# Seven products of quarters for the retention gate, with its operand sums made beside the state-space batches

## The chip, the cores and the metric

The kernel runs on one core of a Trainium2 chip. Time is device microseconds of one execution. The engines are named as in the profile: PE (TensorE matmul), PEld (its weight load), DVE (VectorE), ACT (ScalarE), POOL (GpSimd), and SP, whose queue issues most of the DMA transfers.

## What is computed

Two layers on x of 1024 frames and 1024 channels. The change touches layer 0 only: one input projection `w_in` gives the state-space input u, its gate g_s5, q, k, v and the retention gate g_ret; the two branches are gated and projected back.

```python
h = rmsnorm(x, norm_g[0])
u_s5, g_s5, q, k, v, g_ret = jnp.split(h @ w_in, cuts, axis=-1)
y_s5 = s5_mixer(u_s5, ...)            # diagonal complex recurrence, then a GLU
y_s5 = y_s5 * jax.nn.silu(g_s5)
y_ret = retention(q, k, v) * jax.nn.silu(g_ret)
x = x + jnp.concatenate([y_s5, y_ret], axis=-1) @ w_out
```

Layer 1 is a convolution module of its own, and a last rmsnorm follows.

## The kernel before, in words

All products are made from split operands: a float32 value is a high part in a rounded format (`wh`, `xh`) and the remainder (`wl`, `xl`), and `mm3` (L264) adds three matmuls, high by high, high by low and low by high. A weight block of 1024 x 128 takes one DMA, one cast on ACT (L260) and one subtraction for the low part (L261); the set `LO_V` says for which blocks that subtraction is on DVE, all others are on POOL. Weights are taken in the order of `plan`, two blocks ahead (`wnext`), and have three buffers each for `wf`, `wh` and `wl`. The tiles of x, scaled by the norm's weights, stay in SBUF as 16 pairs `xh`, `xl`: 8 blocks of channels (the depth of the products) by two halves of 512 frames. The norm's factor per frame is in the tile R and is multiplied in when a result leaves its bank.

In `layer0_front` the blocks of u come first. Then 16 blocks of gate (g8 to g15 for the state space, g16 to g23 for the retention) are interleaved with eight state-space batches, two blocks to a batch. A gate block is 2 x 24 matmuls into two PSUM banks, a product with R on DVE, a Silu on ACT and a store. A batch B is, on PE: the input products v (L971), the kernel products kp (L980, L982), and the outputs y of the batch before (L1053, L1057). POOL makes its tables ahead of time (`s5_tables`: Tc and Ts, rotations, and W3, powers; L871 to L873, 12 operations a batch); W3 has two buffers, so its writing waits for the outputs of two batches before. DVE makes the weights W2 of the input products and runs the recurrence; kernel and outputs go through DRAM (`k_d`, `y_d`). Behind the gate come the key, query and value projections (k0, q0, v), which read the 16 pairs of x again.

The order of instructions on an engine is a scheduler's, which puts a ready instruction into a gap; `ORDER` and `s5_order` pin pairs of instructions. On the chip each engine takes its queue strictly in that order. `glu_sums` and `y_pass` (retention stage) already do for the GLU product what the change does for the gate.

Of the kernel before, what the change touches and what calls it, by code (L numbers as in the profile page):

```python
# [19 lines left out]
P = 128  # L20
# [69 lines left out]
def s5_order():  # L90

    seq = []
    for b in range(8):
# [7 lines left out]
        seq += [*kern, *turns, *z[:6]] if b else [*turns, *z[:6], *kern]  # L101
        if b:
# [3 lines left out]
        seq += [(f"gt_{h}", 0), *([(f"wl_g{g + 2}", 0)] if b < 7 else []), (f"gt_{h}", 1)]  # L106
    return [*(("Activation", (f"pw0_{b + 1}", 0), (f"gt_{8 + 2 * b}", 0)) for b in range(1, 7)),
# [15 lines left out]
def nat(ap):  # L123

    return ap.rearrange("p (a c) -> p a c", a=LANES)
# [16 lines left out]
class Trunk:  # L142
# [22 lines left out]
    def plan(self):  # L165
# [4 lines left out]
        seq += [(A["w_ab"][nb], f"g{nb}") for nb in range(8, 24)]  # L170
        for p in range(4):
            seq += [(A["w_ab"][28 + p], f"k{p}"), (A["w_ab"][24 + p], f"q{p}")]
# [6 lines left out]
        quad = lambda i, j, m: A["w_glu"][i, m, :, j]  # L179
        sums = lambda n, m: self.ws_d[n // 2, m, :, n % 2]  # L180
# [110 lines left out]
    def run(self):  # L291
# [29 lines left out]
        self.x1_d = dt("x1_d", [D, T])  # L321

# [28 lines left out]
    def layer0_front(self, st):  # L351
# [155 lines left out]
        self.s5_tables(0)  # L507
        for nb in range(8, 24):
# [7 lines left out]
            w = self.wnext(f"g{nb}")  # L516
            with self.tc.issue_after(self.s5_turn.ins) if nb % 2 == 0 and B else nullcontext():
                gate_block(nb, w, self.gs_d if nb < 16 else self.gr_d)
# [139 lines left out]
    def s5_params(self, sp, tp):  # L658
# [27 lines left out]
        prm = load("s5_prm", (3, NP))  # L686
# [163 lines left out]
        self.bb = [sp.tile([P, NP, 16], F32, name=f"s5_bb{c}") for c in "ri"]  # L850
# [27 lines left out]
    def s5_turned(self, pool):  # L878
# [9 lines left out]
        t = self.mid.tile([P, 4, P], F32, name="turned")  # L888
# [177 lines left out]


# [928 lines left out]
def layout(inp):  # L1996
# [7 lines left out]
    order = np.concatenate([w[:, 0:1024][:, s5p], w[:, 1024:2048][:, s5p], w[:, 4096:5120], w[:, 2048:3072]],  # L2004
                           axis=1)
    A["w_ab"] = _blocks(order)
    A["w_u01"] = np.ascontiguousarray(A["w_ab"][:2].reshape(2, P, 2, 4, P).transpose(2, 1, 3, 0, 4)).reshape(2, P, KB, P)
# [49 lines left out]
```

## Time and profile before

| | us |
|---|---|
| three runs | 1121.92, 1123.55 (median), 1124.43 |
| the profiled execution | 1123.15 |
| its span, first to last instruction | 1121.3 |
| eight batches with their gate blocks | 90.30 to 307.50 |

The trace is of one execution, so its time stands beside the span: 1.85 us lie outside it. A line of the timeline has start, duration, engine, source line, operation, output <- input; a line of the grouped view has the count, busy time and mean ns, then the idle time of the engine before them and who ended it. Matmuls overlap: a busy time of 0.38 us is not their pace, which is read from their starts.

### The profile page before, as it was taken

What the parts mean: (1) busy time and instruction counts of PE and PEld (TensorE: products, weight loads), DVE (VectorE), ACT (ScalarE), POOL (GpSimd) and SP (SyncE); (2) the same over time, 40 slices, a digit from 0 to 9 for tenths busy, and PEclk for the clock granted to TensorE, in tenths of its full rate; (3) what the DMA queues carried; (4) which work ended last, traced back from release to release, by engine and by line L of the source; (5) the groups of instructions that cost most, each with busy time, mean ns of one, the idle gap of its engine ahead of it and who ended that gap; (6) DMA issues with size and microseconds to landing.
All of it is one profiled execution on the core that took longest, in us unless ns stands there. A gap on an engine that the chain in (4) does not pass through costs nothing.

```text
span 1121.3 us, 17174 instructions
## 1 busy us (share of the span) xinstructions
PE 1111.2 (99%) x6254; PEld 976.4 (87%) x6254; DVE 822.5 (73%) x1483; ACT 496.6 (44%) x729; POOL 593.5 (53%) x410
## 2 busy tenths in 40 slices
PE   9999999999999999999999999999999999999997
PEld 8888888888888889989888888888888888888886
DVE  7886877666527469587679433599999899999744
ACT  7313333333233231333456424455535677446773
POOL 3049975552145253232573110689544468779863
PEclk9999999999999999999999999999999999999999
DMA  8346755554498676859998997666678655357965
GB/s 323 114 132 181 212 184 174 174 177 145 137 305 294 232 230 175 314 171 349 395 383 290 358 311 268 219 214 210 234 255 298 244 176 183 123 189 233 331 230 182
DMA packets 125445, 261.99 MB, mean 234 GB/s; under 512 B 19760, under 2 KB 49328, under 8 KB 124720
## 3 DMA queue, kind: packets, MB, share of 16 engines
q1 hardware_dynamic: 121376, 248.04, 65.8%
q10 hardware_dynamic: 3984, 12.85, 3.0%
q8 instruction: 49, 0.80, 0.3%
q14 instruction: 36, 0.29, 0.1%
HBM read 182.53 MB, written 74.12 MB: 229 GB/s over the span
## 4 chain that ended last, share of the span: by engine, by line
PE 90%; DVE 3%; DMA 2%; ACT 2%; issue 1%; SPq 1%; POOL 0%; POOLq 0%; ACTq 0%; DVEq 0%
PE mm_g L271 7%; PE mm_g L272 7%; PE mm_g L273 7%; PE mm_wo L271 5%; PE mm_wo L273 5%; PE mm_wo L272 5%; PE mm_b L272 2%; PE mm_a L272 2%; PE mm_a L271 2%; PE mm_b L271 2%; PE mm_b L273 2%; PE mm_a L273 2%; PE mm_u L273 2%; PE mm_u L271 2%; PE mm_u L272 2%; PE mm_glu L271 2%
## 5 line engine op out<-in xcount | busy, mean ns | idle before, releaser
L1669 DVE SCALAR_TENSOR_TENSOR cv<-u,convw,cv 128x512 f32<-128x512 f32 x390 | 267.9, 750 | 6.0 <-ACT cv L1636 3.9
L1630 POOL TENSOR_TENSOR tp<-tp,tp 128x512 f32<-128x512 f32 x64 | 82.3, 1287 | 33.5 <-ACT tp L1629 32.6
L271 PE MATMUL mm_g<-xh,wh_g 128*128 128x512 f32 x256 | 97.7, 382 | 0.0
L272 PE MATMUL mm_g<-xl,wh_g 128*128 128x512 f32 x256 | 97.0, 379 | 0.0
L273 PE MATMUL mm_g<-xh,wl_g 128*128 128x512 f32 x256 | 95.9, 379 | 0.0
L533 POOL TENSOR_TENSOR s1q<-s1q,s1q 128x512 f32<-128x512 f32 x12 | 17.4, 1447 | 81.2 <-ACT s1q L528 81.2
L1629 ACT ACTIVATE tp<-u,convw 128x512 f32<-128x512 f32 x64 | 45.3, 718 | 31.4 <-POOL tp L1630 30.5
L273 PEld LDWEIGHTS mm_g<-xh,wl_g 128*128 128x128 f32 x256 | 48.4, 189 | 6.9
L271 PEld LDWEIGHTS mm_g<-xh,wh_g 128*128 128x128 f32 x256 | 48.4, 189 | 6.8 <-issue 0.2
L272 PEld LDWEIGHTS mm_g<-xl,wh_g 128*128 128x128 f32 x256 | 48.4, 189 | 6.7
L482 DVE TENSOR_TENSOR gt<-mm_g,R 128x512 f32<-128x512 f32 x32 | 21.9, 686 | 43.7 <-PE mm_g L273 43.7
L272 PE MATMUL mm_oc<-zl,wh_woc 128*128 128x512 f32 (+1 forms) x144 | 51.4, 357 | 0.2 <-DVE zl L1384 0.2
L273 PE MATMUL mm_oc<-zh,wl_woc 128*128 128x512 f32 (+1 forms) x144 | 51.0, 357 | 0.0
L271 PE MATMUL mm_oc<-zh,wh_woc 128*128 128x512 f32 (+1 forms) x144 | 51.0, 363 | 0.0
L271 PE MATMUL mm_g<-h1h,wh_cg 128*128 128x512 f32 x128 | 48.9, 382 | 0.0
L271 PE MATMUL mm_wo<-ysh,wh_wos 128*128 128x512 f32 x128 | 48.9, 382 | 0.0
L273 PE MATMUL mm_b<-h1h,wl_cb 128*128 128x512 f32 x128 | 48.5, 379 | 0.0
L271 PE MATMUL mm_a<-h1h,wh_ca 128*128 128x512 f32 x128 | 48.5, 379 | 0.0
L273 PE MATMUL mm_g<-h1h,wl_cg 128*128 128x512 f32 x128 | 48.5, 379 | 0.0
L272 PE MATMUL mm_wo<-ysl,wh_wos 128*128 128x512 f32 x128 | 48.5, 379 | 0.0
L273 PE MATMUL mm_wo<-ysh,wl_wos 128*128 128x512 f32 x128 | 48.5, 379 | 0.0
L272 PE MATMUL mm_a<-h1l,wh_ca 128*128 128x512 f32 x128 | 48.5, 379 | 0.0
(524 smaller groups left out, 3517.7 us busy)
## 6 DMA issues: line engine op xcount, KB each, us to landing
wf_g<-w_ab SPq DMA_DIRECT2D x16, 512.0 KB
wf_wos<-w_out SPq DMA_DIRECT2D x16, 512.0 KB
wf_wor<-w_out SPq DMA_DIRECT2D x16, 512.0 KB
wf_cb<-w_c SPq DMA_DIRECT2D x16, 512.0 KB
wf_ca<-w_c SPq DMA_DIRECT2D x16, 512.0 KB
wf_woc<-w_out_c SPq DMA_DIRECT2D x16, 512.0 KB
wf_v<-w_v SPq DMA_DIRECT2D x12, 512.0 KB
wf_cg<-w_c SPq DMA_DIRECT2D x11, 512.0 KB
```

The costliest lines, as they stand in the source:

```text
L271: nc.tensor.matmul(ps, wh[:, kb, :], xh, start=start, stop=False, **more)
L272: nc.tensor.matmul(ps, wh[:, kb, :], xl, start=False, stop=False, **more)
L273: self.last_mm = nc.tensor.matmul(ps, wl[:, kb, :], xh, start=False, stop=stop, **more)
L482: nc.vector.tensor_tensor(nat(gt[:, c]), un(ps[:]), nat(self.R[:, c]), op=ALU.mult)
L533: nc.gpsimd.tensor_tensor(a, a, sq[:], op=ALU.add)
L1629: nc.scalar.mul(sk[:], u[:, k:k + HALF], cw[:, nb, k:k + 1])
L1630: gp.tensor_tensor(s0[:], s0[:], sk[:], op=ALU.add)
L1669: v.scalar_tensor_tensor(dst[:], *tap, accs_[i][:], op0=ALU.mult, op1=ALU.add)
```

## The change

The retention gate's 1024 x 1024 x 1024 product is cut into quarters (half the channels in, half out, half the frames) and made with seven products of quarters in place of eight, in the form of Strassen and Winograd. Sums of quarters of the weight (four, `gate_sums`, on DVE, during batches 0 to 3) and of quarters of x (four, `x_sums`, on POOL, during batches 1 to 3) are loaded, made and stored to DRAM (`wr_d`, `tx_d`). In batches 4 to 7 `gate_cube` runs 28 quarter products of 12 matmuls, three or four where a gate block stood. Each weight quarter (14 loads, ra to rn) is split like a weight block. Since SBUF has no room for the sums of x beside x itself, `t_load` writes their high and low parts (ACT, POOL) over tiles of x that are not needed any more, through two buffers `tf`, and `restore` loads x again behind the last use and makes both parts anew (ACT, DVE). Partial results are copied to SBUF by ACT (`p1`, `s2`, `s3`), put back into a bank (`us`) for more products to be added to, or added by DVE at the end (`out`).

To make room, three tables of the state space move to pools that are given back early, and the temporary o of `outer` has one buffer. In `s5_order` the pins of the retention gate's steps go. The weights' columns are laid out anew on the host, with the retention gate as its own array `w_gr`.

```diff
@@ plan
-        seq += [(A["w_ab"][nb], f"g{nb}") for nb in range(8, 24)]
+        seq += [(A["w_ab"][nb], f"g{nb}") for nb in range(8, 16)]
+        gr = [q for m in range(2) for q in (quad(0, 0, m), quad(0, 1, m))]
+        gr += [q for m in range(2) for q in (sums(0, m), sums(2, m), quad(1, 1, m))]
+        gr += [sums(n, m) for m in range(2) for n in (3, 1)]
+        seq += [(q, f"r{chr(97 + i)}") for i, q in enumerate(gr)]
@@ layer0_front
+                if 0 < B < 4:
+                    self.x_sums(B - 1)
+                    if B == 3:
+                        self.x_sums(3)
+                if B < 4:
+                    self.gate_sums(B)
-                gate_block(nb, w, self.gs_d if nb < 16 else self.gr_d)
+                if nb < 16:
+                    gate_block(nb, self.wnext(f"g{nb}"), self.gs_d)
+                else:
+                    cube = cube or self.gate_cube(uv)
+                    next(cube)
+            if nb >= 16:
+                for _ in range(3 - nb % 2):
+                    next(cube)
@@ outer
-            t = self.s5.tile([P, 4, 9 * 16], F32, name=f"o_{B}", tag="tmpP", bufs=2)[:, :, :n]
+            t = self.s5.tile([P, 4, 9 * 16], F32, name=f"o_{B}", tag="tmpP", bufs=1)[:, :, :n]
@@ new
+    def x_sums(self, k):
+        nc, gp = self.nc, self.nc.gpsimd
+        b = [[self.s5.tile([P, HALF], F32, name=f"xs{i}{h}_{k}", tag="s", bufs=8) for h in range(2)] for i in range(2)]
+        for i in range(2):
+            for h in range(2):
+                nc.sync.dma_start(b[i][h][:], self.A["xT"][k + 4 * i, :, h * HALF:(h + 1) * HALF])
+                nc.scalar.mul(b[i][h][:], b[i][h][:], self.vec(V_NG0, k + 4 * i))
+        (b11, b12), (b21, b22) = ((t[:] for t in q) for q in b)
+        gp.tensor_tensor(b22, b22, b12, op=ALU.subtract)
+        gp.tensor_tensor(b12, b12, b11, op=ALU.subtract)
+        gp.tensor_tensor(b11, b22, b11, op=ALU.add)
+        gp.tensor_tensor(b21, b21, b11, op=ALU.subtract)
+        for i in range(2):
+            for h in range(2):
+                nc.sync.dma_start(self.tx_d[k + 4 * i, :, h * HALF:(h + 1) * HALF], b[i][h][:])
+    def gate_sums(self, g):
+        nc, v = self.nc, self.nc.vector
+        m, c = g // 2, slice(g % 2 * 4, g % 2 * 4 + 4)
+        q = [[self.s5.tile([P, HALF], F32, name=f"rs{i}{j}_{g}", tag="s", bufs=8) for j in range(2)] for i in range(2)]
+        fl = "p k n -> p (k n)"
+        for i in range(2):
+            for j in range(2):
+                nc.sync.dma_start(q[i][j][:], self.A["w_gr"][i, m, :, j, c].rearrange(fl))
+        (a11, a12), (a21, a22) = ((t[:] for t in r) for r in q)
+        v.tensor_tensor(a22, a21, a22, op=ALU.add)
+        v.tensor_tensor(a21, a11, a21, op=ALU.subtract)
+        v.tensor_tensor(a11, a22, a11, op=ALU.subtract)
+        v.tensor_tensor(a12, a12, a11, op=ALU.subtract)
+        for i in range(2):
+            for j in range(2):
+                nc.sync.dma_start(self.wr_d[i, m, :, j, c].rearrange(fl), q[i][j][:])
+    def gate_cube(self, uv):
+        nc, v, gp = self.nc, self.nc.vector, self.nc.gpsimd
+        half = lambda h: slice(h * HALF, (h + 1) * HALF)
+        nw = iter(range(14))
+        wn = lambda: self.wnext(f"r{chr(97 + next(nw))}")
+        xq = lambda k0, h: [self.xs[h][k] for k in range(k0, k0 + 4)]
+        b11, b21, b12, b22 = xq(0, 0), xq(4, 0), xq(0, 1), xq(4, 1)
+        def t_load(slot, k0, h):
+            for i, (hi, lo) in enumerate(slot):
+                f = self.s5.tile([P, HALF], F32, name=f"tf{k0}{h}_{i}", tag="tf", bufs=2)[:]
+                nc.sync.dma_start(f, self.tx_d[k0 + i, :, half(h)])
+                nc.scalar.copy(hi[:], f)
+                gp.tensor_tensor(lo[:], f, hi[:].bitcast(F32), op=ALU.subtract)
+        def restore(slot, k0, h):
+            for i, (hi, lo) in enumerate(slot):
+                f, g = self.s5.tile([P, HALF], F32, name=f"xf{k0}{h}_{i}", tag="tf", bufs=2)[:], self.vec(V_NG0, k0 + i)
+                nc.sync.dma_start(f, self.A["xT"][k0 + i, :, half(h)])
+                nc.scalar.mul(hi[:], f, g)
+                v.scalar_tensor_tensor(lo[:], f, g, hi[:].bitcast(F32), op0=ALU.mult, op1=ALU.subtract)
+        def product(ps, w, a, x, more):
+            for k in range(4):
+                self.mm3(ps[:], w, 4 * (a % 2) + k, tuple(t[:] for t in x[k]), k == 0 and not more, k == 3, more)
+        def out(i, a, h, src, add=None):
+            gt = uv.tile([P, HALF], F32, name=f"gr{i}{h}_{a}", tag="ut", bufs=2)
+            r = self.R[:, half(h)]
+            if add is None:
+                v.tensor_tensor(nat(gt[:]), un(src[:]), nat(r), op=ALU.mult)
+            else:
+                v.tensor_tensor(nat(gt[:]), un(src[:]), un(add[:]), op=ALU.add)
+                v.tensor_tensor(gt[:], gt[:], r, op=ALU.mult)
+            nc.scalar.activation(gt[:], gt[:], AF.Silu)
+            nc.scalar.dma_start(self.gr_d[(4 * i + a) * P:(4 * i + a + 1) * P, half(h)], gt[:])
+        part = lambda n, a: self.s5.tile([P, HALF], F32, name=f"r{n}_{a}", tag="s", bufs=8)
+        p1, s2, s3 = {}, {}, {}
+        for m in range(2):
+            w1, w2 = wn(), wn()
+            for a in (2 * m, 2 * m + 1):
+                c = self.bank(f"mm_rc{a}", aux=False)
+                product(c, w1, a, b11, False)
+                p1[a] = part("p1", a)
+                nc.scalar.copy(p1[a][:], c[:])
+                yield
+                product(c, w2, a, b21, True)
+                out(0, a, 0, c)
+                yield
+            if m == 0:
+                t_load(b12, 0, 0)
+        t_load(b11, 4, 1)
+        t_load(b21, 4, 0)
+        t2, t3, t4 = b12, b11, b21
+        for m in range(2):
+            us = {}
+            for n, x in ((2, t2), (3, t3), (4, t4)):
+                w = wn()
+                for a in (2 * m, 2 * m + 1):
+                    if n == 2:
+                        us[a] = self.bank(f"mm_ru{a}", aux=False)
+                        nc.scalar.copy(us[a][:], p1[a][:])
+                    u = us[a]
+                    product(u, w, a, x, True)
+                    if n < 4:
+                        s = (s2, s3)[n - 2]
+                        s[a] = part(f"s{n}", a)
+                        nc.scalar.copy(s[a][:], u[:])
+                    else:
+                        out(1, a, 0, u)
+                    yield
+                if m:
+                    if n == 2:
+                        t_load(b12, 0, 1)
+                    else:
+                        restore(x, 0 if n == 3 else 4, 0)
+        for m in range(2):
+            w1, w2 = wn(), wn()
+            for a in (2 * m, 2 * m + 1):
+                c = self.bank(f"mm_rd{a}", aux=False)
+                product(c, w1, a, b12, False)
+                out(1, a, 1, c, s3[a])
+                yield
+                product(c, w2, a, b22, True)
+                out(0, a, 1, c, s2[a])
+                if a == 3:
+                    restore(b12, 0, 1)
+                yield
```

In the new rows the names are: xs, the quarters of x that are summed; wl_r*, low parts of the weight quarters; xl and xh, the parts of x or of a sum of x in its place, with tf the loaded sum; mm_rd, a bank of the last eight products.

GpSimd at the start of batch 1's table (W_1 is read by that batch's kernel products), before:

```order
L871 TENSOR_TENSOR o_1311<-s_e2i,s_e1i 128x4x128
L872 TENSOR_TENSOR Tc_1308<-s_e2r,s_e1r 128x512
L873 TENSOR_TENSOR Tc_1308<-Tc_1308,o_1311 128x512
L871 TENSOR_TENSOR o_1315<-s_e2i,s_e1r 128x4x128
L872 TENSOR_TENSOR Ts_1309<-s_e2r,s_e1i 128x512
L873 TENSOR_TENSOR Ts_1309<-Ts_1309,o_1315 128x512
```

and now:

```order
L895 TENSOR_TENSOR o_1329<-s_e2i,s_e1i 128x4x128
L896 TENSOR_TENSOR Tc_1326<-s_e2r,s_e1r 128x512
L1101 TENSOR_TENSOR xs_0_1467<-xs_0_1467,xs_0_1465 128x512
L897 TENSOR_TENSOR Tc_1326<-Tc_1326,o_1329 128x512
L1102 TENSOR_TENSOR xs_0_1465<-xs_0_1465,xs_0_1464 128x512
L895 TENSOR_TENSOR o_1333<-s_e2i,s_e1r 128x4x128
L896 TENSOR_TENSOR Ts_1327<-s_e2r,s_e1i 128x512
L1103 TENSOR_TENSOR xs_0_1464<-xs_0_1467,xs_0_1464 128x512
L897 TENSOR_TENSOR Ts_1327<-Ts_1327,o_1333 128x512
L1104 TENSOR_TENSOR xs_0_1466<-xs_0_1466,xs_0_1464 128x512
```

The four differences of the first quarter columns stand inside the table, so its W part comes four operations later.

GpSimd at the table of batch 6, before:

```order
L871 TENSOR_TENSOR o_2621<-s_e2i,s_e1i 128x4x128
L872 TENSOR_TENSOR Tc_2618<-s_e2r,s_e1r 128x512
L873 TENSOR_TENSOR Tc_2618<-Tc_2618,o_2621 128x512
L871 TENSOR_TENSOR o_2625<-s_e2i,s_e1r 128x4x128
L872 TENSOR_TENSOR Ts_2619<-s_e2r,s_e1i 128x512
```

and now:

```order
L896 TENSOR_TENSOR Tc_2822<-s_e2r,s_e1r 128x512
L271 TENSOR_TENSOR wl_rd<-wf_rd,wh_rd 128x1024
L897 TENSOR_TENSOR Tc_2822<-Tc_2822,o_2825 128x512
L895 TENSOR_TENSOR o_2829<-s_e2i,s_e1r 128x4x128
L896 TENSOR_TENSOR Ts_2823<-s_e2r,s_e1i 128x512
L897 TENSOR_TENSOR Ts_2823<-Ts_2823,o_2829 128x512
L271 TENSOR_TENSOR wl_re<-wf_re,wh_re 128x1024
L895 TENSOR_TENSOR o_2833<-s_pi,s_s_ci 128x576
L1142 TENSOR_TENSOR xl_0_143<-tf_0_2680,xh_0_142 128x512
L1142 TENSOR_TENSOR xl_0_156<-tf_1_2684,xh_0_155 128x512
L271 TENSOR_TENSOR wl_rf<-wf_rf,wh_rf 128x1024
```

Weight splits, which were on DVE, and the low parts of the sums of x stand between the operations of the table; the whole W part of the table of batch 5 stands ahead of wl_rd.

TensorE at the input and kernel products of batch 7 (before, a gate block ends, v and kp follow, then y of batch 6):

```order
L273 MATMUL mm_g_1_2852<-xh_1_220,wl_g_2558 128x512
L971 MATMUL v_7_2926<-U_2924,W2r_2912 64x128 x8
L971 MATMUL v_7_2935<-U_2924,W2i_2913 64x128 x8
L980 MATMUL kp_2944<-W_7_2882,s_bdr 32x128 x4
L982 MATMUL kp_2944<-W_7_2882,s_bdi 32x128 x4
```

and now:

```order
L283 MATMUL mm_rd_3130<-xh_1_169,wl_rk 128x512
L281 MATMUL mm_rd_3130<-xh_1_182,wh_rk 128x512
L995 MATMUL v_7_3203<-U_3192,W2i_3181 64x128 x6
L1004 MATMUL kp_3212<-W_7_3150,s_bdr 32x128 x2
L282 MATMUL mm_rd_3130<-xl_1_183,wh_rk 128x512
L283 MATMUL mm_rd_3130<-xh_1_182,wl_rk 128x512
L1004 MATMUL kp_3212<-W_7_3150,s_bdr 32x128 x2
L1006 MATMUL kp_3212<-W_7_3150,s_bdi 32x128 x4
```

The first of the last eight products (quarter rk) is spread among v and kp; its last depth step reads xl_1_183, the last low part of a sum of x that POOL makes. Behind it stand, in this order, y of batch 6, five products, y of batch 7 with one product inside its end, and the key projection with the last product inside its second half.

More of the change, by code (lines that the diff above doesn't have):

```diff
@@ L178, in plan @@
         self.ws_d = self.dram.tile([2, 2, P, 2, KB, P], F32, name="ws_d")
[L179 to L180 removed]
+        quad, sums = quads(A["w_glu"]), summed(self.ws_d)
         glu = [q for m in range(2) for q in (quad(0, 0, m), quad(0, 1, m))]
@@ L321, in run @@
         self.x1_d = dt("x1_d", [D, T])
+        self.tx_d = dt("tx_d", [KB, P, T])
         with ExitStack() as mid:
@@ L849, in s5_params @@
         cfr, cfi = both[:, 0], both[:, 1]
-        self.bb = [sp.tile([P, NP, 16], F32, name=f"s5_bb{c}") for c in "ri"]
+        self.bb = [tp.tile([P, NP, 16], F32, name=f"s5_bb{c}") for c in "ri"]
         bc = lambda q: q.unsqueeze(2).broadcast_to([P, NP, 16])
```

24 lines of the change are left out of this document (16 added, 8 removed).

## The prediction

> **What bounds the kernel now.** I read the page first (share of each engine), then the busy time in the eight stretches of one state-space batch each, then the timelines of TensorE and GpSimd inside them, then single tiles.
>
> ```profile
> span 1121.3 us, 17174 instructions
> PE 1111.2 (99%) x6254; PEld 976.4 (87%) x6254; DVE 822.5 (73%) x1483; ACT 496.6 (44%) x729; POOL 593.5 (53%) x410
> ```
>
> PE is busy for 99% of the span. This alone does not say that fewer products make it faster: the stretches do, because they show who is second.
>
> ```profile
> core 0: us, PE busy (x) PEld busy (x) DVE busy (x) ACT busy (x) POOL busy (x), PEclk, DMA share, GB/s
> 90.30:117.38 27.08, 27.08 (x163) 23.12 (x161) 20.80 (x33) 7.46 (x12) 26.53 (x21) 1.00 0.68 188
> 117.38:144.54 27.16, 27.16 (x194) 23.81 (x193) 20.23 (x30) 10.86 (x19) 26.60 (x19) 1.00 0.70 219
> 144.54:171.70 27.16, 27.16 (x194) 23.82 (x193) 19.23 (x29) 8.79 (x16) 16.49 (x12) 1.00 0.54 181
> 171.70:198.86 27.16, 27.16 (x194) 23.82 (x193) 19.23 (x29) 8.78 (x16) 16.51 (x12) 1.00 0.54 176
> 198.86:226.02 27.16, 27.16 (x193) 23.82 (x193) 19.27 (x29) 8.77 (x16) 16.54 (x12) 1.00 0.55 178
> ...
> 253.20:280.30 27.10, 27.10 (x193) 23.79 (x192) 18.49 (x29) 8.72 (x16) 6.40 (x5) 1.00 0.42 137
> 280.30:307.50 27.20, 27.20 (x193) 23.82 (x192) 13.68 (x22) 6.57 (x10) 4.74 (x2) 1.00 0.42 142
> sum 217.20, PE 217.20 PEld 189.83 DVE 150.14 ACT 68.76 POOL 130.35; mean PE 27.15 PEld 23.73 DVE 18.77 ACT 8.59 POOL 16.29
> ```
>
> Each row is a batch. PE never waits in any of them. POOL is as full as PE in batches 0 and 1 (26.5 of 27.1 us) and runs ahead later: it makes the tables of batches 1 to 7 and must deliver each before that batch's kernel products.
>
> **What the change takes away.** These rows show the pace of the gate's matmuls (68 steps from the first to the second), a batch's fixed part, and the end of the gate before the key projection.
>
> ```profile
> 102.39 0.38 PE L271 MATMUL mm_g<-xh,wh_g 128*128 128x512 f32 x1
> 117.07 0.38 PE L273 MATMUL mm_g<-xh,wl_g 128*128 128x512 f32 x1
> 119.27 0.43 PE L980 MATMUL kp<-W,s_bdr 128*32 128x128 f32 x8
> 119.52 0.40 PE L982 MATMUL kp<-W,s_bdi 128*32 128x128 f32 x8
> 119.85 2.06 PE L1053 MATMUL y<-S,W 64*128 64x128 f32 x32
> 123.64 0.46 PE L271 MATMUL mm_g<-xh,wh_g 128*128 128x512 f32 x1
> 311.30 0.46 PE L271 MATMUL mm_k<-xh,wh_k 128*128 128x512 f32 x1
> ```
>
> (117.07 - 102.39) / 68 = 0.216 us a matmul. The retention gate has 8 blocks x 2 halves x 8 (depth) x 3 (high and low parts) = 384 of them, seven products of quarters have 7 x 4 x 4 x 3 = 336: 48 fewer, a gain of 48 x 0.216 = 10.4 us if PE still never waits. One quarter product (12 matmuls) is 2.59 us, one batch's outputs y 123.64 - 119.85 = 3.79 us, its kernel products kp 0.58 us.
>
> **What it puts on POOL.** Three kinds of work are new there: 16 differences of x (batches 1 to 3), 16 low parts of the sums of x, and the low parts of the 14 weight quarters, which DVE made for the 8 blocks before (the names r* are not among those sent to DVE). Rows for POOL: the first operation of batch 1's table, two behind it, the last table operation, its waits in that time, and the nearest rows for what is new.
>
> ```profile
> 100.43 1.39 POOL L871 TENSOR_TENSOR o<-s_e2i,s_e1i 128x512 f32<-128x512 f32 x1
> 101.78 1.41 POOL L872 TENSOR_TENSOR Tc<-s_e2r,s_e1r 128x512 f32<-128x512 f32 x1
> 103.27 1.29 POOL L873 TENSOR_TENSOR Tc<-Tc,o 128x512 f32<-128x512 f32 x1
> 262.94 1.42 POOL L873 TENSOR_TENSOR W<-W,o 128x576 f32<-128x576 f32 x1
> L872 POOL TENSOR_TENSOR W<-s_pr,s_s_cr 128x576 f32<-128x576 f32 x8 | 9.8, 1223 | 46.0 <-PE y L1053 46.0
> L1384 POOL TENSOR_TENSOR zl<-co,zh 128x512 fp32r<-128x512 f32 x11 | 14.1, 1281 | 3.0 <-ACT zh L1382 3.0
> L261 POOL TENSOR_TENSOR wl_glu<-wf_glu,wh_glu 128x1024 fp32r<-128x1024 f32 x14 | 33.2, 2380 | 21.3 <-ACT wh_glu L260 21.3
> ```
>
> Before, tables 1 to 7 run from 100.43 to 264.36 with 46.0 us of waiting: 117.9 us of work. New: 32 x 1.28 + 14 x 2.38 = 74.3 us. In the eight stretches POOL would come to 130.35 + 74.3 = 204.7 us, while PE's time shrinks to 217.2 - 10.4 = 206.8. That is full, and the order lets nothing slide: in GpSimd's new order the last low part of the seventh product's first block stands behind all tables and behind 12 of the 14 weights, and PE has 0.4 us (two matmuls), 0.4 (rest of kp), 3.79 (y of batch 6), five products 12.95, 3.79 (y of batch 7) and two products 5.18 behind it: 26.6 us up to where the key projection stands alone (one product is moved in among the key's; I count it here).
>
> **The sum**, from POOL's start of table 1, which nothing moves:
> - 100.4 + 117.9 (tables) + 20.5 (x differences) + 20.5 (x low parts) + 12 x 2.38 = 28.6 (weights): 287.9.
> - Contention with DVE. A weight split on DVE and the table operation beside it:
>
> ```profile
> 157.57 1.95 DVE L261 TENSOR_TENSOR wl_g<-wf_g,wh_g 128x1024 fp32r<-128x1024 f32 x1
> 158.52 2.15 POOL L873 TENSOR_TENSOR Tc<-Tc,o 128x512 f32<-128x512 f32 x1
> L261 DVE TENSOR_TENSOR wl_g<-wf_g,wh_g x16: 1214/1216/2324, 77.0 to 293.4; 128x1024 fp32r<-128x1024 f32 x16
> ```
>
>  DVE needs 1.95 in place of 1.21, POOL 2.15 in place of 1.29: it loses 0.86 us to a DVE operation with two operands in SBUF. Two such meetings go with the later gate splits (-1.7), one comes since POOL is no longer idle where a split falls (+0.9): -0.9, bounds -1.7 and +0.9. The 16 weight sums that batches 0 to 3 gain on DVE are of that kind and half as long: 16 x 0.43 = +6.9, bounds 0 and 16 x 0.61 = 9.8. The Trainium skill (SBUF — State Buffer, section "SBUF: two separate sides") says that the pair of ports shared by VectorE and GpSimd is an exclusive lock, held for a whole instruction. By that rule each sum would hold POOL off for its full 0.61 us, and the total below would be 2.9 us more; the row above shows a loss of 0.86 where the rule would allow 1.21, so I stay with the row.
> - The temporary o has one buffer in place of two, so each of 28 writes of it waits for the operation before. An operation without such a wait starts 1.35 us after one of 1.39, one with it 1.49 after one of 1.41: 0.12 x 28 = +3.4, bounds 0 and 3.4. I take 3.4, since the wait stands in the order.
> - Waits of POOL for data. These rows are two loads of 256 KB, from issue to the copy that reads them:
>
> ```profile
> 93.36 0.60 SPq L911 DMA_DIRECT2D PTr<-pt_d  x1
> 95.30 0.60 SPq L911 DMA_DIRECT2D PTi<-pt_d  x1
> 99.42 0.59 ACT L915 COPY pw<-PTr 128x512 f32<-128x512 f32 x1 [4.15 <-DMA PTr<-pt_d]
> 103.32 0.59 ACT L915 COPY pw<-PTi 128x512 f32<-128x512 f32 x1 [3.31 <-DMA PTi<-pt_d]
> ```
>
>  6.1 and 8.0 us. The x differences enter POOL's queue from about 103.3, and their loads are issued among these, behind 1 MB of weight quarters; the sums of x pass through two buffers, so the third tile waits for a load issued only when the first is used, with 2.6 to 3.7 us of other POOL work between. I take +4 (one microsecond at the first place, 3.5 and 2.4 less covered parts at the first two sets of sums, none at the last two), bounds 0 and 17.
>
> Total 287.9 - 0.9 + 6.9 + 3.4 + 4 = 301.3, plus 26.6 = 327.9, against 311.3: **+16.6 us**. The profiled execution took 1123.15 (its span and 1.85 around it), 0.4 under the median: 1139.8, so **1140**. With all bounds at the low end the end is 312.8 (+1.5), at the high end 345.6 (+34). A measurement can tell about 0.2% (2.2 us).
>
> **Edits that I cost at nothing.** ACT gains 66 copies and casts; at the 0.59 of the copies above and twice that for the six more weights that is some 43 us, over 217 in which it is busy 68.76. DVE gains 16 sums, 12 restored tiles of x and 8 more gate steps, and loses 8 splits of 1.2 to 2.0: it has 67 us free. If ACT's cover were gone, the saved partial sums would be late: each has one other product (2.59 us) between its end and the next use of its bank. The tables moved to other pools change no time: GpSimd's first table waits for the same loads of x as before. PE's early stalls come to some 3 to 6 us: the table for the kernel products of batch 1 was ready at 116.4 for products at 119.3 and 119.5, and four differences of 1.28 now stand ahead of it.
>
> ```profile
> 114.95 1.42 POOL L873 TENSOR_TENSOR W<-W,o 128x576 f32<-128x576 f32 x1
> ```
>
> These stalls are inside the POOL total, not on top of it, since POOL is late anyway.
>
> **Rivals.**
> 1. POOL keeps up and the change is faster. For it: 46 us of POOL's waiting lie in this stretch. Against: the new work is 74.3. Break-even needs POOL's last low part by 311.3 - 26.6 = 284.7, the full gain by 274.3; the work alone, without any contention or wait, ends at 286.2. It decides only if the new operations cost some 10 us less than the nearest rows. Time 1123.2 - 10.4 = 1112.8.
> 2. The additions cost only their bare work: contention, self-waits and late data all hide in each other. +1.5 to +2: 1125, no difference that can be told.
> 3. The transfers of batches 0 to 3 decide. The change loads and stores 8 MB of x and 8 MB of weight sums there. In one later stretch the 16 engines moved 352 GB/s at a share of 0.97, so 16 MB are 44 us of all engines; the shares of the four rows above (0.68, 0.70, 0.54, 0.54 of 27.1) are 66.7 us, together 111 in 108.6. Then each set of differences holds POOL, in whose queue it stands, 4 to 6 us more: 4 x 5 on top of the forecast, 1160.
>
> ```profile
> 500.00:600.00 100.00, 99.72 (x624) 89.57 (x623) 70.07 (x135) 47.70 (x75) 55.21 (x31) 1.00 0.97 352
> ```
>
> **How the numbers follow.** Forecast (POOL bound, +3 to +30) 0.80; rival 1 0.05; rival 2 0.06; rival 3 0.09. The forecast and rival 3 are slower by over 0.2%: 0.89; same 0.06; faster 0.05. The range leaves out rivals 1 to 3 beyond its ends and the outer bounds of the unknown costs: 1128 to 1153.
>
> **What would show it.** Right: POOL over 95% busy from batch 0 to the last gate product; PE idle before kp of batch 1 (released by W), before products of the quarters rd and rg (released by wl), and before the first product of quarter rk (released by xl), together some 27 us; 48 fewer matmuls; GpSimd's Tc operations of 2.15 us gone in tables 6 and 7, and longer ones in batches 0 to 3. Wrong: PE idle under 8 us in all, or idle released by DMA or ACT, or the key projection starting before 311.

## The result and the profile after

| | before | after |
|---|---|---|
| median, us | 1123.24 (1121.92 to 1124.43) | 1174.58 (1171.25 to 1176.48) |
| profiled execution and its span, us | 1123.15, 1121.3 | 1174.5, 1172.4 |
| key projection starts, us | 311.30 | 361.26 |

The ratio is 1.0454, with a 95% interval of 1.0428 to 1.0481: 51.3 us slower. Forecast were 1140 and a range that ended at 1153. The page's head after:

```profile
span 1172.4 us, 17492 instructions
PE 1123.5 (96%) x6206; PEld 979.5 (84%) x6206; DVE 849.4 (72%) x1511; ACT 537.1 (46%) x795; POOL 671.2 (57%) x456
```

There are 48 matmuls fewer, and yet PE is busy 12.3 us longer. The windows show where. Of before, from the first batch to the key projection, and batches 0 to 3 alone:

```profile
90.30:311.30 221.00, 221.00 (x1555) 193.51 (x1553) 150.83 (x230) 70.81 (x117) 132.71 (x95) 1.00 0.54 174
90.30:198.86 108.56, 108.56 (x739) 94.57 (x737) 79.48 (x120) 35.90 (x61) 86.13 (x63) 1.00 0.61 191
```

Of after, from the first batch to the key projection, and batches 0 to 3 alone (the input products of batch 4 start at 230.85):

```profile
90.30:361.26 270.96, 232.02 (x1498) 194.93 (x1497) 175.29 (x251) 107.40 (x178) 207.10 (x141) 0.93 0.75 236
90.30:230.85 140.55, 119.86 (x743) 102.60 (x741) 101.47 (x136) 46.66 (x78) 119.06 (x84) 0.93 0.85 270
```

The columns are the stretch, its length, busy time of PE, PEld, DVE, ACT and POOL, the granted clock, the DMA share and GB/s. The stretch grew by 49.96 us, nearly the whole loss. PE sat idle for 270.96 - 232.02 = 38.94 us. It ran 57 matmuls fewer there (48 are saved, and the 12 of the last product stand inside the key projection, behind this end; the rest are edges), which is 12.3 us at 0.216, and was busy for 11.02 more all the same: 23.3 us went into matmuls that ran slower. So 38.9 + 23.3 - 12.3 = 49.9. The granted clock of the same row, 0.93 in place of 1.00, says nearly as much: 0.07 x 270.96 = 19 us. Batches 0 to 3 take 140.55 us in place of 108.56, with the 16 DMA engines busy 0.85 of the time in place of 0.61; POOL has 207.10 of 270.96 us, 76%.

What PE waited for in that stretch (the waits: us in total, times, longest):

```profile
PE mm_rc L281 <- ACT rp L1174: 5.9, 2, 5.7
PE v L995 <- DVE W2r L945: 5.5, 2, 4.2
PE mm_g L283 <- DVE wl_g L271: 5.1, 2, 2.8
PE mm_rd L281 <- DVE gr L1161: 4.8, 2, 4.5
PE v L995 <- issue: 4.8, 1, 4.8
PE mm_ru L281 <- ACT rs L1197: 4.7, 1, 4.7
PE y L1081 <- ACT W L1060: 3.2, 1, 3.2
PE mm_rd L281 <- ACT wh_rk L270: 2.8, 1, 2.8
PE mm_g L281 <- DVE gt L493: 2.1, 1, 2.1
```

Thirteen pauses, 38.9 us, and POOL is the releaser of none. The pace after one of them, on PE's timeline:

```profile
253.93 0.79 PE L281 MATMUL mm_rc<-xh,wh_rb 128*128 128x512 f32 x1 [5.66 <-ACT rp L1174]
254.51 0.63 PE L282 MATMUL mm_rc<-xl,wh_rb 128*128 128x512 f32 x1
254.94 0.63 PE L283 MATMUL mm_rc<-xh,wl_rb 128*128 128x512 f32 x1
...
257.04 0.38 PE L282 MATMUL mm_rc<-xl,wh_rb 128*128 128x512 f32 x1
257.26 0.38 PE L283 MATMUL mm_rc<-xh,wl_rb 128*128 128x512 f32 x1
```

The matmuls start 0.43 us apart in place of 0.22 until 257.04: seven steps took 3.11 us in place of 7 x 0.216 = 1.51, and this 1.6 comes on top of the pause. The granted clock (the third figure from the end) is half in these steps and full behind them:

```profile
253.93:257.04 3.11, 3.11 (x7) 2.49 (x8) 0.00 (x0) 0.96 (x2) 3.11 (x2) 0.51 0.64 245
257.04:260.00 2.96, 2.96 (x23) 2.27 (x22) 0.69 (x1) 1.85 (x3) 2.80 (x4) 1.00 0.67 226
```

Over all 13 pauses the 23.3 us make 1.8 each.

Who held the releasers? ACT, ahead of that pause:

```profile
244.35 0.58 ACT L1174 COPY rp<-mm_rc 128x512 f32<-128x512 f32 x1
251.40 1.04 ACT L1060 COPY W<-Wd 128x1024 f32<-128x1024 f32 x1 [6.47 <-DMA Wd<-k_d]
...
253.29 1.06 ACT L1174 COPY rp<-mm_rc 128x512 f32<-128x512 f32 x2
```

The copies of partial results, for which PE waits, stand behind the copy of the kernel matrix W, which waited 6.47 us for its transfer (the cast of a weight quarter lies between them). In batches 0 to 3 it is DVE:

```profile
158.89 1.47 DVE L1119 TENSOR_TENSOR rs<-rs,rs 128x512 f32<-128x512 f32 x1 [9.59 <-DMA rs<-w_gr]
160.28 0.68 DVE L493 TENSOR_TENSOR gt<-mm_g,R 128x512 f32<-128x512 f32 x1
...
161.48 0.67 DVE L945 TENSOR_TENSOR W2r<-W2r,pw 128x512 f32<-128x512 f32 x1
```

The first sum of weight quarters waited 9.59 us for its load, with the bank's evacuation (gt) and W2r behind it in the queue. PE, which takes W2r, stood still for 4.24 us up to 162.21. The pause given to "issue" is of this kind, by the times: PE went on at 124.42, when DVE had read (123.64 + 0.67 = 124.31) the bank that v writes, behind a sum that itself had waited 3.37 us:

```profile
122.41 1.31 DVE L1119 TENSOR_TENSOR rs<-rs,rs 128x512 f32<-128x512 f32 x1 [3.37 <-DMA k_d<-Kg]
123.64 0.67 DVE L1049 TENSOR_TENSOR S<-v,d 128x508 f32<-128x508 f32 x1
124.42 1.97 PE L995 MATMUL v<-U,W2r 128*64 128x128 f32 x16 [4.75 <-issue]
```

### The profile page after: what moved, and what is told of

It reads as the page before. It is cut to its first block, busy times and chain, and to the rows that moved or that the text cites. A ratio compares the mean times of both kernels' runs of the same rounds, so it can differ in the third digit from the quotient of the medians.

```text
span 1172.4 us, 17492 instructions
## 1 busy us (share of the span) xinstructions
PE 1123.5 (96%) x6206; PEld 979.5 (84%) x6206; DVE 849.4 (72%) x1511; ACT 537.1 (46%) x795; POOL 671.2 (57%) x456
## 4 chain that ended last, share of the span: by engine, by line
PE 69%; POOL 9%; DMA 8%; DVE 6%; issue 4%; ACT 3%; SPq 1%; POOLq 0%; ACTq 0%; DVEq 0%
PE mm_wo L282 5%; PE mm_wo L281 5%; PE mm_wo L283 5%; PE mm_b L282 2%; PE mm_g L282 2%; PE mm_a L282 2%; PE mm_g L281 2%; PE mm_b L283 2%; PE mm_a L283 2%; PE mm_a L281 2%; PE mm_b L281 2%; PE mm_g L283 2%; PE mm_glu L281 2%; PE mm_glu L282 2%; PE mm_glu L283 2%
## 5 line engine op out<-in xcount | busy, mean ns | idle before, releaser
L557 POOL TENSOR_TENSOR s1q<-s1q,s1q 128x512 f32<-128x512 f32 x12 | 17.5, 1457 | 81.0 <-ACT s1q L552 72.3
L283 PE MATMUL mm_g<-xh,wl_g 128*128 128x512 f32 x128 | 49.6, 392 | 5.1 <-DVE wl_g L271 5.1
L281 PE MATMUL mm_g<-xh,wh_g 128*128 128x512 f32 x128 | 50.6, 395 | 2.1 <-DVE gt L493 2.1
L282 PE MATMUL mm_g<-xl,wh_g 128*128 128x512 f32 x128 | 50.0, 391 | 0.0
L281 PE MATMUL mm_u<-xh,wh_u 128*128 128x512 f32 x128 | 47.4, 382 | 1.2 <-ACT wh_u L270 1.2
L282 PE MATMUL mm_g<-h1l,wh_cg 128*128 128x512 f32 x128 | 48.5, 379 | 0.0
L283 PE MATMUL mm_a<-h1h,wl_ca 128*128 128x512 f32 x128 | 48.5, 379 | 0.0
L281 PE MATMUL mm_b<-h1h,wh_cb 128*128 128x512 f32 x128 | 48.5, 379 | 0.0
```

The lines of the kernel that those rows point to most:

```text
L281: nc.tensor.matmul(ps, wh[:, kb, :], xh, start=start, stop=False, **more)
L282: nc.tensor.matmul(ps, wh[:, kb, :], xl, start=False, stop=False, **more)
L283: self.last_mm = nc.tensor.matmul(ps, wl[:, kb, :], xh, start=False, stop=stop, **more)
L557: nc.gpsimd.tensor_tensor(a, a, sq[:], op=ALU.add)
```

## The experiments

Three theories stood against one another: the prediction's (POOL's work holds the end of the gate), transfers (the sums' 16 MB delay the state space's own loads), and queue order (an engine that takes its queue strictly in order has an instruction at its head that waits for a transfer, with one that PE needs behind it). Times are medians, each set against the runs of before on the same chip.

### Which of the sums, and is it POOL

Without the sums of the weight (the quarters are loaded plain):

```diff
-                if B < 4:
-                    self.gate_sums(B)
...
+        sums = lambda n, m: quad(n // 2, n % 2, m)
```

> Leaves out the sums of the weight's quarters (16 loads, 16 DVE operations, 16 stores, 8 MB): the products that used them load plain quarters in their place, so the gate's values are not the reference's. Theory Q (queues): PE's pauses in batches 0 to 3 (20.7 us) come from DVE's queue, where the first sum of each batch waits for its load while what PE needs stands behind it, and each pause is followed by products at half pace; the whole 50 us is 39.0 of pauses - 10.4 of saved products + 21.4 of slow products, so batches 0 to 3 cost about 20.7 x (1 + 21.4 / 39.0) = 32: 1143 us (1138 to 1150), PE idle under 4 us up to batch 4. Theory P (POOL is the bound, as predicted): only the contention term of 6.9 goes: 1168. Theory D (the 16 MB of transfers): half of the volume, so half of the 32: 1158.

Without the sums of x:

```diff
-                    self.x_sums(B - 1)
-                    if B == 3:
-                        self.x_sums(3)
-                nc.sync.dma_start(f, self.tx_d[k0 + i, :, half(h)])
+                nc.sync.dma_start(f, self.A["xT"][k0 + i, :, half(h)])
```

> Leaves out the sums of x's quarters (16 loads, 16 ACT and 16 POOL operations, 16 stores, 8 MB): the places take plain quarters of x, so the gate's values are not the reference's. Theory Q: DVE's sums still wait for their loads; a little less in front of them on SP's queue: 1160 to 1172. Theory P: 20.5 us of POOL's differences and the waits for their loads go: 1150. Theory D: half of the volume: 1158.

Both edits together:

> Leaves out both kinds of sums (plain quarters in their places, so the gate's values are not the reference's); the seven products, the weight quarters, the loads into the places of x and the restores stay. All three theories expect about 1142 here; what is left against 1123.2 - 10.4 = 1112.8 is the price of batches 4 to 7: by theory Q 18.3 us of pauses and about 10 of slow products, released by ACT (copies of partial results queued behind the copy of the W tile) and DVE: 1141. If POOL is what holds batches 4 to 7, PE's waits there are named wl or xl.

All the work, with the low parts of the 14 weight quarters and of the 16 sums of x on DVE:

```diff
-                gp.tensor_tensor(lo[:], f, hi[:].bitcast(F32), op=ALU.subtract)
+                v.tensor_tensor(lo[:], f, hi[:].bitcast(F32), op=ALU.subtract)
@@ wload: which engine makes wl
+        ... or len(name) == 2 and name[0] == "r"
```

> The whole change, but the low parts of the 14 weight quarters and of the 16 loaded sums of x are made by DVE in place of POOL: 14 x 2.38 + 16 x 1.28 = 53.8 us off POOL, some 14 x 1.21 + 16 x 0.65 = 27 onto DVE. Theory Q: no pause of PE was released by POOL, so no gain: 1170 to 1182. Theory P: 40 us or more less: 1135 or below. Theory D: unchanged, 1174.

| | us | ratio, 95% interval | over before |
|---|---|---|---|
| no weight sums | 1163.90 | 1.0349 (1.0310 to 1.0388) | +40.2 |
| no x sums | 1166.17 | 1.0392 (1.0371 to 1.0413) | +42.5 |
| neither | 1138.89 | 1.0133 (1.0111 to 1.0156) | +15.2 |
| low parts off POOL | 1176.91 | 1.0474 (1.0447 to 1.0502) | +53.2 |

The last row speaks against the POOL theory, which forecast 1135 or below. POOL is freed of 30 of the operations that the prediction added and has 161.89 us of work in 267.40:

```profile
90.30:357.70 267.40, 227.57 (x1495) 192.16 (x1494) 203.15 (x283) 108.60 (x179) 161.89 (x110) 0.94 0.78 245
```

The time does not fall. The work went to DVE, for which PE also waits, but DVE does not hide a gain: it releases 19.1 us of PE's pauses here and 17.5 in the change. In the change the page's chain of work runs over POOL for 9% of the span, with waits for transfers in between, and here for 4%, at the same time.

The sums cost 51.3 - 15.2 = 36.1 us, but dropping one kind gives back 11.1 or 8.8: either kind alone is enough to keep about four fifths of the loss. Without the weight sums POOL does release PE, though not by its work:

```profile
140.10 0.66 PE L1005 MATMUL kp<-W,s_bdi 128*32 128x128 f32 x8 [10.99 <-POOL W L896]
```

POOL's own rows ahead of it:

```profile
137.42 1.26 POOL L1100 TENSOR_TENSOR xs<-xs,xs 128x512 f32<-128x512 f32 x1 [6.32 <-ACT xs L1098]
138.65 1.40 POOL L896 TENSOR_TENSOR W<-W,o 128x576 f32<-128x576 f32 x1
```

A difference of x waits 6.32 us for ACT's scaling of a late load, with the last step of the table's W behind it.

### Transfers alone

After, with the sums' loads and stores as they are, and without their 32 sums and 16 scalings:

```diff
-        gp.tensor_tensor(b22, b22, b12, op=ALU.subtract)
...
-        v.tensor_tensor(a22, a21, a22, op=ALU.add)
...
-                nc.scalar.mul(b[i][h][:], b[i][h][:], self.vec(V_NG0, k + 4 * i))
```

> The whole change, but the 32 operations of the sums on DVE and POOL and the 16 of ACT on x are left out; all 64 transfers of 256 KB stay, each store sending what its load brought, so the gate's values are not the reference's. Theory Q: nothing of DVE, ACT or POOL waits for these loads any more: 1139 to 1147. Theory D (volume): the pauses of batches 0 to 3 stay: 1165 or more. In between, both take part.

Before, with 64 copies of 256 KB within HBM, as many transfers of the same size as the sums have, issued in batches 0 to 3 and read by nobody (each reads and writes HBM, where a load or a store of the sums does one of the two); and with every second of them:

```diff
+    def ballast(self, mark, n):
...
+            with issue_after(mark.ins):
+                nc.sync.dma_start(self.ballast_d[i], self.A["xT"][i % 8, :, half])
```

> The kernel before, with 64 copies of 256 KB from DRAM to DRAM (16 MB, as much as the sums load and store) put into SP's queue behind the loads of PT, BT and U and of Wd of batches 0 to 3; nothing waits for them and they wait for nothing, the computation is the reference's. Theory D (the volume itself makes the loads late that the batches need): the share of the DMA engines goes from 0.58 to about 0.9 there and PE pauses as in the changed kernel: 1140 to 1155. Theory Q (only the work of the sums in the strict queues): no pause, 1123 to 1127. My estimate is 1140, since the run with transfers only kept 29 of the 36 us, but its stores still waited in SP's queue for their loads.

> The same with every second copy, 8 MB. If the engines' share decides, half the volume (share about 0.73) fits beside the rest and costs little: 1123 to 1128, far less than half of the run with 16 MB. If each transfer costs alike, half of it.

The same 64 copies from ACT's queue, behind its copies of pw and W and four of its Silus:

```diff
-                nc.sync.dma_start(self.ballast_d[i], ...)
+                nc.scalar.dma_start(self.ballast_d[i], ...)
```

> The kernel before with the same 16 MB of copies, but issued from ACT's queue (behind its copies of pw and W and a Silu of each of batches 0 to 3), computation as the reference. Theory S (SP's queue: the stores of the kernel k_d stood 14.7 us later in it, behind 17 more issues, and PE paused 14.55 us for them): SP's order is as before, so 1123 to 1130. Theory D (the engines are full whoever issues): again 1145 to 1155, with U, PT, Wd landing late.

After, with the sums' loads issued by ACT and their stores by GpSimd:

```diff
-                nc.sync.dma_start(b[i][h][:], self.A["xT"][...])
+                nc.scalar.dma_start(b[i][h][:], self.A["xT"][...])
-                nc.sync.dma_start(self.tx_d[...], b[i][h][:])
+                nc.gpsimd.dma_start(self.tx_d[...], b[i][h][:])
```

> The whole change with all its work; the 32 loads of the sums are issued from ACT's queue and the 32 stores from POOL's, so that SP's queue holds none of them. Theory S: SP's own loads and stores are no longer behind them, some 20 us go: 1145 to 1160, less whatever ACT's and POOL's queues wait for in their turn. Theory D: unchanged, 1168 to 1180.

| | us | ratio, 95% interval | over before |
|---|---|---|---|
| after, transfers only | 1167.82 | 1.0393 (1.0376 to 1.0411) | +44.8 |
| before and 16 MB | 1151.40 | 1.0248 (1.0233 to 1.0263) | +28.3 |
| before and 8 MB | 1131.87 | 1.0075 (1.0058 to 1.0092) | +8.8 |
| before and 16 MB by ACT | 1146.93 | 1.0213 (1.0197 to 1.0229) | +24.0 |
| after, sums off SP | 1192.88 | 1.0617 (1.0586 to 1.0649) | +69.2 |

Transfers do it with no new arithmetic at all: 28.3 us on before, and on the kernel without sums the transfers add 44.8 - 15.2 = 29.6. Half of it costs a third: the windows of the first 120 us in these two kernels, 16 MB and then 8 MB, show shares of 0.84 and 0.76 (before: 0.58).

```profile
90.00:210.00 120.00, 103.14 (x701) 90.01 (x700) 71.48 (x111) 30.67 (x53) 81.44 (x62) 0.93 0.84 267
```

```profile
90.00:210.00 120.00, 111.97 (x763) 97.85 (x764) 79.17 (x122) 37.27 (x62) 85.41 (x64) 0.97 0.76 244
```

Where it bites is a chain through DRAM. PE's two longest pauses with 16 MB, and SP's queue in the same kernel:

```profile
137.06 3.78 PE L1071 MATMUL y<-U,W 128*128 128x128 f32 x16 [14.55 <-ACT W L1050]
224.33 1.98 PE L983 MATMUL v<-U,W2r 128*64 128x128 f32 x16 [6.10 <-DVE W2r L924]
```

```profile
122.15 5.44 SPq L1009 DMA_DIRECT2D k_d<-Kg  x8
```

and SP's queue of before:

```profile
107.45 3.99 SPq L997 DMA_DIRECT2D k_d<-Kg  x8
```

The kernel goes to `k_d`, is read back as Wd and copied to W by ACT for y. Its stores were issued at 122.15 in place of 107.45, and y waited 14.55 us. With the copies in ACT's queue they were issued in time, but it took SP 10.05 us to issue the same eight:

```profile
108.85 10.05 SPq L1008 DMA_DIRECT2D k_d<-Kg  x8
```

The timeline merges the eight stores with the waits between them. Each store took 0.30 to 0.43 us of the queue, as before, and the eight together 2.8; in the other 7.2 us SP stood until earlier transfers had landed. The packed trace shows why. Every transfer, whether SP or ACT issues it, reports its landing on one of eight semaphores, taken in turn (before: 715 transfers, 89 or 90 to each), and the next with the same one is not issued until that transfer has landed. So at most eight are under way, in before and in the kernels with copies alike. SP's waits for copies that nobody reads and that ACT issued, from 90 to 210 us:

```profile
SPq L914 <- DMA ballast_d<-xT: 21.2, 6, 7.5
SPq L1008 <- DMA ballast_d<-xT: 14.3, 12, 2.7
SPq L258 <- DMA ballast_d<-xT: 12.3, 4, 3.7
```

The lines are issues of the tables PT and BT, of the kernel's stores and of gate weights, none of which needs the copies. All waits of SP's queue for landings in these 120 us come to 12.3 us in before, 34.1 with 8 MB, 44.9 with 16 MB, 81.5 with 16 MB by ACT, and 38.2 in the change; without sums they are 11.3. The transfers themselves also take longer: a store of the kernel landed after 1.67 us in before and after 4.39 with 16 MB from SP (medians of the same 120 us, from the packed trace). So an added transfer can be paid for in three ways: by its place in an issuing queue, by its turn among the eight semaphores, and by its share of the engines. Moving the issue saves 4.3 us of 28.3, but it also puts the copies' own waits into ACT's queue. No run parts the turn from the share; that would take a kernel with more semaphores or with fewer, larger copies.

In the change itself moving the issue was worse, although GpSimd's stores report to eight other semaphores. There a difference of x waits longer still, between the steps of the table's W on POOL, and PE stands for 16.75 us:

```profile
142.38 1.26 POOL L1101 TENSOR_TENSOR xs<-xs,xs 128x512 f32<-128x512 f32 x1 [10.63 <-ACT xs L1099]
```

```profile
149.21 0.65 PE L1006 MATMUL kp<-W,s_bdi 128*32 128x128 f32 x8 [16.75 <-POOL W L897]
```

The Trainium skill (DMA: Bandwidth & Descriptors, section "Issuing engines are not separate DMA queues") says that the queues of all issuing engines share the same 16 engines. The runs fit that, 1151.4 us from SP's queue and 1146.9 from ACT's, but do not prove it, since the two queues also share the eight semaphores.

### What remains without the sums

The +15.2 of the kernel with neither sum come late: none of its pauses is in batches 0 to 3.

```profile
PE mm_rc L282 <- ACT rp L1169: 5.0, 1, 5.0
PE mm_rd L282 <- ACT wh_rk L271: 3.7, 1, 3.7
PE mm_rd L282 <- DVE gr L1156: 3.7, 2, 3.4
PE mm_ru L282 <- ACT rs L1192: 2.4, 2, 1.8
```

All are queue heads of ACT and DVE. Pins were added that put the copies for which PE waits ahead of W's copy and of weight casts (engine, the late one, the early one), to the kernel without sums, and more of that kind:

```diff
+    ('Activation', ('W1_4', 0), ('rp1_2', 0)), ('Activation', ('W1_5', 0), ('rs2_1', 0)),
+    ('Activation', ('W1_6', 0), ('rs3_2', 0)), ('Activation', ('wh_rg', 0), ('rs2_0', 0)),
...
```

> No sums, as in the run without both kinds of sums (plain quarters in their places, so the gate's values are not the reference's), and in ACT's queue the copies of the W tiles of batches 4 to 6 are pinned behind the copies of partial results and the cast of the quarter rk, four further casts likewise. Theory Q (a strict queue, whose head waits for a transfer): of the 14.75 us of PE's pauses left there, 11.1 were released by ACT; with their slow products (24.5 us lost in all, 1.66 a microsecond of pause) 18 us go: 1121 (1118 to 1126). Rival (ACT is simply too full, or the copies themselves are late): 1134 to 1139.

```diff
+    ('DVE', ('xl_6_0', 1), ('gr01_1', 0)), ('DVE', ('xl_7_0', 1), ('gr11_2', 0)),
+    ('SP', ('tf41_0', 0), ('U_5', 0)), ('SP', ('tf41_2', 0), ('U_6', 0)),
...
```

> No sums (plain quarters, so the gate's values are not the reference's), ACT's order as in the run with pinned copies, and besides DVE's last restores of x pinned behind the gate steps that free PE's banks, the loads of U ahead of loads into the places of x, and three more ACT pins. Of the 13.2 us of PE's pauses in the run with pinned copies, 6.6 were released by DVE's gate steps, 3.1 by U and 3.5 by ACT's copies. Theory Q (each pause is a queue's head that waits; put right, the seven products gain): 1120 or below. Rival (the waits only move on, to the next late transfer): 1128 to 1137.

All the work, with the first set of pins, and with each sum put later in its engine's queue:

```diff
+    *(('DVE', (f'rs11_{g}', 0), (f'gt_{9 + 2 * g}', 1)) ...),
+    ('Pool', (f'xs11_{k}', 0), (f'W3_{min(k + 2, 4)}', 3)),
...
```

> The whole change with all its work, in another order: the first sum of a batch's weight quarters is pinned behind that batch's last gate step on DVE, the first difference of x behind the table's last operation on POOL, the scaling of x behind a late Silu on ACT, and ACT's copies as in the run with pinned copies. Theory Q: the loads have landed when the queue comes to them; 1120 to 1135. Theory D: the 16 MB still pass in batches 0 to 4: 1150 or more. Theory P: POOL's work is the same: 1160 or more.

The kernel without sums, and without loads into the places of x and their restoring:

```diff
-            if m == 0:
-                t_load(b12, 0, 0)
-        t_load(b11, 4, 1)
-        t_load(b21, 4, 0)
...
-                        restore(x, 0 if n == 3 else 4, 0)
```

> No sums, and also no loads into the places of x and no restores: the seven products read x's own quarters throughout, so the gate's values are not the reference's; 336 products, 14 weight quarters and the copies of partial results stay. If the loads into the places and the restores (28 of 256 KB, with 28 ACT and 28 POOL or DVE operations) are what holds batches 4 to 7, the seven products now show their gain: 1113 to 1118. If the copies of partial results and the weight quarters hold them, little changes from the run without sums: 1132 to 1139.

That kernel with the pins on ACT, and four buffers in place of two for the outputs gr:

```diff
+    ('Activation', ('W1_4', 0), ('rp1_2', 0)), ('Activation', ('W1_5', 0), ('rs2_1', 0)),
+    ('Activation', ('W1_6', 0), ('rs2_3', 0)), ('Activation', ('W1_7', 0), ('wh_rn', 0)),
...
+            pool, tag = ((uv, "ut"), (self.s5, "tf"))[(i + h) % 2]
```

> As the run with the products alone (plain quarters, no sums, no loads into the places, no restores; the gate's values are not the reference's), and in ACT's queue the copies of the W tiles of batches 4 to 7 stand behind the copies of partial results (W of batch 7 behind the cast of the last quarter), and the gate's output tiles have four places in place of two. Theory Q2 (in batches 4 to 7 ACT's head waits for Wd, with the copies that free PE's banks behind it, and the output tiles wait for their stores): PE's 11.45 us of pauses there and their slow products go to 3 or less, 1113 to 1121, below the kernel before. Rival (one copy between a bank's end and its next use is too tight in any order): 1128 to 1134.

| | us | ratio, 95% interval | over before |
|---|---|---|---|
| no sums, pins | 1135.19 | 1.0120 (1.0082 to 1.0158) | +12.2 |
| no sums, more pins | 1140.16 | 1.0150 (1.0131 to 1.0169) | +17.0 |
| all work, sums late | 1169.39 | 1.0415 (1.0384 to 1.0445) | +46.4 |
| products only | 1133.05 | 1.0091 (1.0075 to 1.0107) | +10.1 |
| products only, pins, four buffers | 1115.25 | 0.9934 (0.9920 to 0.9947) | -7.3 |

Order alone gave nothing that can be told as long as the places of x were loaded and restored (the intervals of +15.2, +12.2 and +17.0 overlap): the waits moved on. The queue theory had forecast 1121 and 1120 or below for the two rows, and 1120 to 1135 for all work with the sums late, which took 1169.39; there PE waited 28.7 us for ACT, DVE and late loads of U, and 5.5 for POOL. With more pins they are at

```profile
PE mm_ru L298 <- ACT rs L1208: 5.8, 1, 5.8
PE mm_q L298 <- DVE gr L1172: 3.1, 1, 3.1
```

the last one behind the gate, as is another of 2.5 us. The products alone are still slower than before, by the same two heads, W's copy on ACT and the outputs gr on DVE:

```profile
216.52 1.04 ACT L1055 COPY W<-Wd 128x1024 f32<-128x1024 f32 x1 [5.44 <-DMA Wd<-k_d]
...
218.42 1.06 ACT L1169 COPY rp<-mm_rc 128x512 f32<-128x512 f32 x2
```

With the pins and the buffers PE does not wait once in the gate,

```profile
210.00:310.00 100.00, 99.94 (x679) 84.99 (x678) 62.72 (x97) 45.09 (x71) 64.98 (x39) 1.00 0.63 201
```

and only then the 48 matmuls show as time: 7.3 us of the 10.4 (8.1 in the span of the profiled execution). This kernel lacks the sums and the places of x, so it is no version of the change; of those that do all the work, the one with the sums late has the lowest median, 1169.39, with an interval that overlaps that of the change.

The loss in steps, each against its own runs of before: all +51.3; without sums +15.2 (36.1 less); without loads into places and restoring +10.1 (5.1 less); with order and buffers -7.3 (17.4 less). How much of the 17.4 is order and how much buffers was not parted.

## Why the prediction was wrong

- **Slower, and from this stretch: right, but not for the reason given.** POOL, which was to make it slower, released none of PE's pauses. Right were the 48 matmuls (6254 to 6206).
- **"That is full, and the order lets nothing slide": the step that failed.** The forecast let POOL's last low part of a sum of x set the end of the gate. POOL's work was right in size: 132.71 + 74.3 = 207.0 us up to the key projection, and 207.10 measured. But "full" took PE's time as fixed. The stretch became 271 us long and POOL idle for 63.9 of it. The three largest of its waits:

```profile
POOL xs L1101 <- ACT xs L1099: 15.1, 3, 8.8
POOL wl_rn L271 <- ACT wh_rn L270: 11.2, 1, 11.2
POOL xl L1142 <- ACT xh L1141: 9.0, 4, 5.7
```

 At the sums and their low parts that is 24.1 us, where the sum had +4 "for data", bounds 0 and 17. So the last low part ended at 324.4 in place of 301.3. Even so PE never waited for it: with the 26.6 us reckoned behind it, POOL would have let the key projection start at 351.0, and it started at 361.26. PE was held by ACT and DVE instead, and these, in the rows shown above, by late transfers. Whether POOL's work would bind at +16.6 once all other waits are gone was not tried; no run shows it.
- **Rival 3, the transfers (chance 0.09, 1160): the nearest of the four.** Its reckoning, 111 us of transfers in 108.6, was near: 0.85 of 140.55 us is 119. Wrong were the place, POOL's differences of x, and the price, 20 us on top. With no sums made at all these transfers cost 29.6 of the sums' 36.1 us, and on before 28.3 with nobody reading them, by what they do to the transfers of others (`k_d`, Wd, U, PT).
- **"Edits that I cost at nothing": the second term that failed.** ACT's copies were priced by their duration (43 us in 217 with 69 busy), and their cover by one other product, 2.59 us. But ACT is held at a queue head for 5 to 6 us at a time, so the cover is gone, and DVE's outputs wait for their two buffers. In the kernel with products only ACT released 6.0 us of PE's 11.4 us of pauses and DVE 5.4; order and buffers together gave back 17.4 us. DVE's sums of the weight took 0.69 to 1.87 us each, where 0.61 was reckoned.
- **PE's pauses were priced at their own length.** "Together some 27 us" of idle time had nothing for the slow matmuls behind them: 23.3 us here, 0.6 of the idle time again.
- **PE's early stall at kp of batch 1 for W: not in the change.** In other kernels POOL does release kp: for 17.9 us without the weight sums, for 35.4 with the sums' loads and stores off SP, for 2.2 with the sums late. At the longest pause of the first two a difference of x that waited for its load stood ahead of W. So the place was right, and the cause a late load and not the four differences' own time.

Open is how the 36.1 us divide between the two kinds of sums: taken out one at a time they are worth 11.1 and 8.8, and the remaining 16.2 come back only when both are out. Open too is by which of the three ways the transfers are paid for.

## What to carry to other kernels

Where one engine is 99% busy, ask of each added instruction which queue it enters, what transfer can hold it at the head, and which instruction that the busy engine needs stands behind: free time on an engine is no cover by itself. Price added transfers by the DMA share of their own stretch (from 0.61 to 0.85 here), by how many may be under way at once and what their issues wait for, and by the shortest chain through DRAM in it, and measure that with transfers that nobody reads before the arithmetic is written. Try the pure saving first, with every addition left out: if that is already slower, order and buffers come before the rest.

## What the runs showed of the hardware

- Half pace after short pauses. Pauses of 2.5 us and more were mostly followed by matmuls 0.43 us apart in place of 0.22, for about 1.7 to 3 us of loss; single ones of 1.75 us (products only) and 2.33 us (all work, sums late) were followed by the full pace, but two of 2.13 and 2.37 us in a row, in the change, by the half. In the packed trace of the change the granted clock is 0.5 in nine stretches of 3.41 or 6.83 us between 90 and 362 us, 37.5 us in all, and 1.0 otherwise; in before it is 1.0 there. The Trainium skill (TensorE: Matmul & The Clock Gate, section "What's actually happening") gives half the clock after an idle window of about 3.4 us. The half agrees with the rows; the pauses that set it off here are shorter.
- The cost of transfers that nobody reads is far from proportional: 8 MB in 120 us cost 8.8 us, 16 MB 28.3.
- Issuing did not get slower with the DMA engines at a share of 0.83 (16 MB by ACT, 90 to 210 us): each of the kernel's eight stores took 0.30 to 0.43 us of SP's queue, as before. What grew, from 3.99 to 10.05 us, is the waiting between them for earlier transfers to land.
